# A fast-matrix MLP in an encoder layer: second half product by product, summed in PSUM; first half with the next group's operands combined ahead

## The chip, the cores and the metric

The kernel runs on one core of one Trainium2 chip, in one launch. The metric is device time in microseconds, as the median of several runs. A profile of one execution gives the trace that is read here. The engines are TensorE (PE in the trace; its weight loads are PEld), VectorE (DVE), ScalarE (ACT), GpSimd (POOL) and SyncE (SP), which issues nearly all DMAs here.

## The reference, cut to what matters

One encoder layer on 2048 prompt tokens and 256 sample tokens, width 1024: an adaptive-norm modulation, one input projection, dilated attention on half of the heads, RWKV-7 mixing on the other half, an output projection, and then the MLP that this change is about (`D_FF` is 4096):

```
x = x + gt1 * (concatenate([attn, rw]) @ w_out)
h = rmsnorm(x, g_norm2) * (1 + sc2) + sh2
x = x + gt2 * (square(relu(h @ w_ff1)) @ w_ff2)
```

## The kernel before, in words

All is float32. A product that must be exact enough is made of three float32r matmuls: each operand is split into a high part (a ScalarE copy to float32r) and a low part (the value less the high part), and high*high, high*low and low*high are summed in PSUM.

The kernel has four phases; the last two matter here. `phase_c` makes the output projection, the residual, the second norm, and the first half of the MLP (`h @ w_ff1`). `phase_d` makes the second half (`... @ w_ff2`) and the second residual. Both halves use Winograd's form of Strassen's method: each matrix is cut into 2 x 2 blocks, seven products of block combinations stand in for eight block products, and additions put the results together.

The 2304 tokens are cut into three groups of 768, each of two halves of 384 (`GROUPS`, line 2625). The order in which instructions stand on each engine's queue is written out by a planner (`Pace`, lines 70 to 258): each part of the work is a stream (a generator), which yields what it waits for and which engine it uses next. The planner keeps a rough clock with estimated costs, always lets the stream go on whose next step could start first, and so fixes one order per engine; SP's DMAs are ordered in the same way. On the chip each engine and SP then run their queue strictly in that order, with semaphores for what they wait for. `room(name, n)` stands for one of n buffers of a name coming free, `take` takes one, `drop` gives it back.

**First half, in `phase_c`.** For each group, and for each of 16 passes p (one 128-row block of each half of the 4096 hidden columns), `up_stream` (line 2260) makes the seven products, 12 matmuls of 384 columns each. The moving operands `HS[0..6]` (tiles `hs0h`, `hs0l`, ... in the trace) are combinations of the four blocks of the group's h2 (128 x 1536 in SBUF each), made once per group: `hload_stream` (line 2153) loads the blocks for each of the seven combinations anew from HBM, 14 loads of 768 KB through three buffers `hr`; `hpart_stream` (line 2170) adds or subtracts them on VectorE (seven additions per group) and copies the high part on ScalarE, once the group before has used that operand for the last time; `hlow_stream` (line 2187) makes the low part on VectorE. There is one set of `HS`, shared by the groups. `part_stream` and `low_stream` prepare the weight combinations (`s`, `mh`, `ml`, `mx`, `xn`; lows on GpSimd). `sum_up_stream` (line 2285) reads the products out of PSUM, mostly on VectorE, applies relu and square, and makes the seven left operands of the second half, which go to HBM as `gs`. The four result banks of a pass are used twice within it: products 4, 5 and 6 wait until products 0, 2 and 3 have been read.

**Second half, in `phase_d`.** The inner dimension of each block product (2048 rows) is cut into four quarters q of four 128-row blocks. The loop runs over groups g, then q, then the seven products i (`TURNS`, line 2384): 84 turns. A turn has a left operand (384 tokens x 512 rows, loaded from `gs` as `sr` by `left_load`, split by `left_part` into `s`: high on ScalarE, low on VectorE) and a right operand (512 rows x 512 columns, high and low in a tile `t`, two buffers). `right_load` (line 2419) loads the four blocks of `w_ff2` for each (g, q), 1 MB each, tiles `b`; `right_part` (line 2431) combines them with four VectorE subtractions and copies the seven high parts on ScalarE; `right_low` (line 2490) makes the low parts on GpSimd. As g is the outer loop, all right operands are made three times. `down_stream` (line 2501) runs the turn's 36 matmuls of 512 columns: three PSUM banks (128 tokens each), 12 matmuls per bank. `add_stream` (line 2519) reads each bank and copies it (q = 0) or adds it to the accumulators `acc[0..6]` in SBUF. After the fourth quarter `out_stream` (line 2555) combines the accumulators of the seven products into the four blocks of the result (`acc` + `acc` on VectorE), multiplies by the gate (VectorE), adds the residual `xr` (GpSimd) and stores. `finish_load` (line 2535) loads the gates and the residuals.

Of the kernel before, what the change touches and what calls it, by code (L numbers as in the profile page):

```python
# [18 lines left out]
D = 1024  # L19
# [242 lines left out]
def hymba_layer(ctx, tc, A, out_p, out_s, scratch):  # L262
# [1675 lines left out]
    def phase_c(pc):  # L1938
# [11 lines left out]
        first = ExitStack()  # L1950
# [22 lines left out]
        def gate(i, rg):  # L1973
            z, turn = take(wp, [128, D], FT, f"gate{rg}", 1)
            g = S["gates"]
            dma(z, bass.AP(tensor=g.tensor, offset=g.offset + (i * 2 + rg) * D, ap=[[0, 128], [1, D]]))
            gates[i, rg] = z, turn
# [95 lines left out]
        def sum_stream():  # L2073
            for b in BL:
                for h in range(2):
# [4 lines left out]
                    z, t = take(wp, [128, 512], FT, "z", 2)  # L2080
# [42 lines left out]
        def scale_stream():  # L2123
            for b in BL:
                rg = int(b >= SP // 128)
                yield room("hf", 2), "V"
                hf, t = take(wp, [128, KD, 128], FT, "hf", 2)
# [10 lines left out]
            ended.add("scale")  # L2138

# [12 lines left out]

        def hload_stream():
            for g in range(3):
                for th in range(2):
                    yield (*(lambda b=b: b in hs_ and hs_[b].t is not None for b in GROUPS[g][th]), "S")
                for i, parts in enumerate(MOVING):
                    if i == 4 and not g:
                        yield at("pool"), "S"
                    for j, part in enumerate(parts):  # L2160
                        yield room("hr", 3), "S"
                        z, turn = take(hp, [128, 4, 384], FT, "hr", 3)
                        kh, th = BLOCKS[part.strip("-")]
                        for c0, b0, n in RUNS[g][th]:
                            dma(z[:, :, c0:c0 + n], S["h2"][4 * kh:4 * kh + 4, :, b0:b0 + n].rearrange("k p t -> p k t"))
                        raws["h", g, i, j] = z, turn
                        mark(at("raw", "h", g, i, j), 4200.0)
                        yield

        def hpart_stream():  # L2170
            for g in range(3):
                for i, parts in enumerate(MOVING):
                    yield at("raw", "h", g, i, 0), (lambda: not g or (g - 1, NP - 1, i) in through), "V"
                    z, turn = raws.pop(("h", g, i, 0))
                    for j, part in list(enumerate(parts))[1:]:
                        yield at("raw", "h", g, i, j), "V"
                        y, t1 = raws.pop(("h", g, i, j))
                        tt(y, z, y, OP.subtract if part[0] == "-" else OP.add)
                        drop(turn)
                        z, turn = y, t1  # L2180
                    yield "A"
# [547 lines left out]
```

## Time and profile before

| | |
|---|---|
| median of 3 runs | 4220.1 us (4215.66 to 4223.14) |
| profiled execution, its own time | 4224.25 us |
| its span, first to last instruction | 4222.4 us, mean granted TensorE clock 0.95 |
| TensorE matmul busy | 3861.4 us (91%) |
| VectorE, ScalarE, GpSimd busy | 3218.9 (76%), 1995.5 (47%), 2143.1 us (51%) |
| DMA | 651.33 MB, 154 GB/s over the span |
| passes of the first MLP half | from about 2611 to 3390 us of the span |
| second half | from about 3393 us to the end |

In the rows of the trace, nearly every compute instruction has line L119, since the planner's wrapper issues it; so groups are told apart by their tiles (`out<-in`), their shape and their engine. A group's row gives busy time, mean ns of one, and the idle time of that engine just before such instructions with what ended it. Buffer numbers are left out of tile names. "issue" is time in which the engine waited for nothing that the profile shows.

### The profile page before, as it was taken

What the parts mean: (1) busy time and instruction counts of PE and PEld (TensorE: products, weight loads), DVE (VectorE), ACT (ScalarE), POOL (GpSimd) and SP (SyncE); (2) the same over time, 40 slices, a digit from 0 to 9 for tenths busy, and PEclk for the clock granted to TensorE, in tenths of its full rate; (3) what the DMA queues carried; (4) which work ended last, traced back from release to release, by engine and by line L of the source; (5) the groups of instructions that cost most, each with busy time, mean ns of one, the idle gap of its engine ahead of it and who ended that gap; (6) DMA issues with size and microseconds to landing.
All of it is one profiled execution on the core that took longest, in us unless ns stands there. A gap on an engine that the chain in (4) does not pass through costs nothing.

```text
span 4222.4 us, 77051 instructions
## 1 busy us (share of the span) xinstructions
PE 3861.4 (91%) x28986; PEld 3181.1 (75%) x28986; DVE 3218.9 (76%) x5708; ACT 1995.5 (47%) x4437; POOL 2143.1 (51%) x1760
## 2 busy tenths in 40 slices
PE   8989999997999999999999798997979979889897
PEld 5878878887666666666666577997979967677675
DVE  4898888798668668767667355888888867988978
ACT  5556556555565565566455222333333333333232
POOL 2564442122545645545544444775757745565654
PEclk9999999999899999899799899998989999999999
DMA  6566555454423323324222475546564464454543
GB/s 228 196 223 236 182 193 191 151 195 156 128 75 103 107 61 107 100 69 123 78 64 60 165 247 172 174 166 220 166 211 153 153 217 153 151 190 151 194 151 110
DMA packets 492837, 651.33 MB, mean 154 GB/s; under 512 B 160688, under 2 KB 363440, under 8 KB 491440
## 3 DMA queue, kind: packets, MB, share of 16 engines
q1 hardware_dynamic: 491632, 645.72, 47.4%
q8 instruction: 228, 3.74, 0.4%
q14 instruction: 145, 1.19, 0.1%
q10 hardware_dynamic: 832, 0.69, 0.1%
HBM read 447.83 MB, written 198.46 MB: 153 GB/s over the span
## 4 chain that ended last, share of the span: by engine, by line
PE 42%; DVE 9%; issue 4%; POOL 3%; DMA 2%; ACT 2%; SPq 0%; DVEq 0%; POOLq 0%; ACTq 0%
PE p L119 30%; PE pb L119 5%; PE pc L119 3%; PE ps L119 3%; POOL t L119 2%; DVE acc L119 2%; DMA hr<-scr_h 2%; PE pt L119 1%; DVE s L119 1%; DVE mb L119 1%; DVE hr L119 1%; DVE t L119 0%; DVE b L119 0%; DVE m L119 0%; DMA mx<-scr_mix 0%
## 5 line engine op out<-in xcount | busy, mean ns | idle before, releaser
L119 PE MATMUL p<-t,s 128*128 128x512 f32 x3024 | 720.1, 399 | 94.5 <-POOL t L119 61.4
L119 PEld LDWEIGHTS p<-t,s 128*128 128x128 f32 x3024 | 578.8, 193 | 235.7 <-POOL t L119 75.7
L119 PE MATMUL pin<-hi,whi 128*128 128x386 f32 (+3 forms) x1512 | 495.6, 328 | 4.8 <-ACT praw L327 3.5
L119 PE MATMUL pin<-hi,wlo 128*128 128x386 f32 (+3 forms) x1512 | 481.0, 318 | 1.6 <-POOL wlo L119 1.6
L119 PE MATMUL pin<-lo,whi 128*128 128x386 f32 (+3 forms) x1512 | 481.2, 318 | 0.9 <-DVE lo L119 0.9
L119 POOL TENSOR_TENSOR t<-b,t 128x2048 fp32r<-128x2048 f32 x60 | 294.3, 4906 | 176.7 <-ACT t L119 176.7
L119 ACT ACTIVATE s<-sr 128x1536 fp32r<-128x1536 f32 x84 | 125.0, 1488 | 467.3 <-PE p L119 399.2
L119 PEld LDWEIGHTS pin<-hi,whi 128*128 128x128 f32 x1512 | 289.7, 192 | 15.8 <-issue 6.1
L119 PEld LDWEIGHTS pin<-lo,whi 128*128 128x128 f32 x1512 | 290.7, 192 | 4.4 <-DVE lo L119 1.8
L119 PEld LDWEIGHTS pin<-hi,wlo 128*128 128x128 f32 x1512 | 289.9, 192 | 2.6 <-POOL wlo L119 2.6
L119 PE MATMUL ps<-kz,q 128*128 128x512 f32 (+2 forms) x400 | 272.8, 775 | 0.8 <-DVE st L119 0.6
L119 POOL TENSOR_TENSOR sql<-sq,sqh 128x384 fp32r<-128x384 f32 (+1 forms) x104 | 123.8, 1191 | 289.9 <-DVE sqh L119 239.9
L119 POOL TENSOR_TENSOR wlo<-raw,whi 128x512 fp32r<-128x512 f32 x118 | 180.2, 1531 | 166.6 <-ACT whi L327 161.3
L119 POOL TENSOR_TENSOR x<-x,msk 128x512 f32<-128x512 f32 x144 | 172.2, 1204 | 173.8 <-ACT x L119 156.1
L119 POOL TENSOR_TENSOR sw<-uv,wc 64x128 f32<-64x128 f32 x288 | 121.8, 423 | 244.5 <-DVE uv L119 220.0
L119 DVE CUSTOM_DVE_ANT_0 p<-ps,tb 128x256 f32<-128x256 f32 (+2 forms) x400 | 129.7, 362 | 80.9 <-PE ps L119 53.0
L119 DVE TENSOR_TENSOR acc<-acc,p 128x512 f32<-128x512 f32 x189 | 125.5, 681 | 84.2 <-PE p L119 83.9
L119 ACT ACTIVATE p<-p,st 128x256 f32<-128x256 f32 (+2 forms) x384 | 172.8, 453 | 27.9 <-DVE st L119 26.4
L119 DVE TENSOR_TENSOR s<-sr,s 128x1536 fp32r<-128x1536 f32 x84 | 154.3, 1837 | 37.6 <-ACT s L119 37.6
L119 DVE TENSOR_TENSOR u<-u,p 128x384 f32<-128x384 f32 x192 | 106.4, 554 | 100.3 <-PE p L119 90.2
L119 POOL TENSOR_TENSOR t<-t,t 128x2048 fp32r<-128x2048 f32 x24 | 117.6, 4900 | 109.4 <-ACT t L119 109.4
L119 PE MATMUL pb<-kr,bk 64*128 64x128 f32 x1152 | 156.9, 299 | 0.8 <-DMA bk<-scr_bk 0.3
(446 smaller groups left out, 10952.4 us busy)
## 6 DMA issues: line engine op xcount, KB each, us to landing
scr_gs<-gs SPq DMA_DIRECT2D x336, 192.0 KB
sr<-scr_gs SPq DMA_DIRECT2D x84, 768.0 KB
x<-wff SPq DMA_DIRECT2D x96, 512.0 KB
b<-wff SPq DMA_DIRECT2D x48, 1024.0 KB
whi<-scr_wp SPq DMA_DIRECT2D x54, 512.0 KB
wlo<-scr_wp SPq DMA_DIRECT2D x54, 512.0 KB
hr<-scr_h SPq DMA_DIRECT2D x34, 768.0 KB
raw<-wada SPq DMA_DIRECT2D x83, 256.0 KB
```

The source lines that it names most:

```text
L119: return f(out, *a, **k)
```

## The change: what it does

**Second half.** The loops are turned around: the product i is now the outermost, then the group g, then the quarter q. The right operands of a product (four quarters) are made once and kept for all three groups: five buffers `t`, of which one can be filled ahead, and each of the others once the third group's turn has used the old one. Their blocks are loaded for each product as it needs them, through three buffers `b` (14 block loads per q over the seven products, 56 in all), with 28 VectorE additions. The four quarters of a product are summed in PSUM: the three banks of an (i, g) stay open over four turns and are read once. The combining is done while reading: two accumulators for all tokens (`X`, `W`, nine tiles of 128 x 512 each) hold the partial sums, and products 1, 4, 5 and 6 each finish one block of the result for all groups, which is gated, added to the residual and stored at once. The products come in another order, so `PLACE` and the order of `gs` change with it. The loads of gates and residuals wait for the first product, and residuals come in single tiles with four buffers.

**First half.** For groups 1 and 2, `hload_stream` loads each of the four blocks once, into buffers taken from two pools; `hpart_stream` makes three combinations before the group before has ended (`t1`, `t2`, and b22 - b12 in b12's place) and a fourth, `t4`, after the first operand has been copied; the high-part copies still wait for the last use of the old operand. The buffers for the second pool come from a pool of the output projection (gates, `z`, `hf`), moved to a pool of its own, `zC`, that is closed when the norm is done.

```diff
+        zp = second.enter_context(tc.tile_pool(name="zC", bufs=1, side="right", reuse_waits="tile"))
...
+            yield at("summed"), "V"
+            second.close()
+            late["more"] = pc.enter_context(tc.tile_pool(name="mC", bufs=1, side="right", reuse_waits="tile"))
+            mark(at("more"))
...
+        HR = [("hr", n) for n in ("b11", "b12", "t1")] + [("hm", n) for n in ("b22", "b21", "t2")]
...
+            yield at("more"), "S"
+            for g in (1, 2):
+                if g == 2:
+                    yield at("t4", 1), "S"
...
+                for where, n in HR:
+                    yield room(where, 3), "S"
+                    raws["h", g, n] = take(hp if where == "hr" else late["more"], [128, 4, 384], FT, where, 3)
+                    if n in BLOCKS:
+                        hload(raws["h", g, n][0], g, n)
+                    mark(at("raw", "h", g, n), 4200.0)
+                    yield
...
+            for g in (1, 2):
+                yield (*(at("raw", "h", g, n) for n in ("b11", "b12", "b22", "b21", "t1", "t2")), "V")
+                r = {n: raws.pop(("h", g, n)) for _, n in HR}
+                tt(r["t1"][0], r["b12"][0], r["b11"][0], OP.subtract)
+                yield "V"
+                tt(r["t2"][0], r["b22"][0], r["t1"][0], OP.subtract)
+                yield "V"
+                tt(r["b12"][0], r["b22"][0], r["b12"][0], OP.subtract)
+                yield
+                for i, n in enumerate(("b11", "t2", "b12", "t1", "b21", "t4", "b22")):
+                    if i == 1:
+                        yield room("hr", 3), "V"
+                        r["t4"] = take(hp, [128, 4, 384], FT, "hr", 3)
+                        tt(r["t4"][0], r["b21"][0], r["t2"][0], OP.subtract)
+                        mark(at("t4", g))
+                    yield (lambda: (g - 1, NP - 1, i) in through), "A"
+                    act(HS[i][0], r[n][0], AF.Copy)
...
-        TURNS = [(g, q, i) for g in range(3) for q in range(4) for i in range(7)]
-        acc = [dp.tile([128, 3, 512], FT, name=f"acc{i}") for i in range(7)]
+        TURNS = [(i, g, q) for i in range(7) for g in range(3) for q in range(4)]
+        RIGHT = [("b11",), ("b21",), ("b22", "-b12", "b11"), ("b12", "-b11"), ("b22", "-b12"), ("b22",),
+                 ("b21", "-b22", "b12", "-b11")]
+        DONE = {1: (0, 0), 4: (1, 1), 5: (0, 1), 6: (1, 0)}
+        X, W = (dp.tile([128, 9, 512], FT, name=n) for n in "xw")
...
         def right_part():
+            for i in range(7):
                 for q in range(4):
+                    yield at("raw", i, q, 0), "V"
+                    z, turn = raws.pop((i, q, 0))
+                    for j, part in list(enumerate(RIGHT[i]))[1:]:
+                        yield at("raw", i, q, j), "V"
+                        y, t1 = raws.pop((i, q, j))
+                        tt(y, z, y, OP.subtract if part[0] == "-" else OP.add)
+                        drop(turn)
+                        z, turn = y, t1
+                    yield room("t", 5), "A"
+                    w, t = take(dp, [128, 2, 4, 512], FR, "t", 5)
+                    act(w[:, 0], z, AF.Copy)
...
         def down_stream():
+            for i, g, q in TURNS:
+                yield at("s", i, g, q), at("t", i, q), "P"
...
+                    if q == 0:
+                        yield room("p", 8), "P"
+                        pp[i, g, k] = take(psum, [128, 512], FT, "p", 8)
...
+                        mm(ps, s[:, 0, r, ks], w[:, 0, r], start=q == 0 and r == 0, stop=False, skip_group_check=True)
...
+                if g == 2:
+                    drop(t1)
...
         def out_stream():
+            for i in range(7):
+                for g in range(3):
+                    for k in range(3):
+                        x, w = X[:, 3 * g + k], W[:, 3 * g + k]
+                        yield at("p", i, g, k), "V"
+                        ps, turn = pp.pop((i, g, k))
+                        if i == 0:
+                            copy(x, ps)
+                        elif i == 2:
+                            tt(x, x, ps, OP.add)
+                        elif i == 3:
+                            tt(w, x, ps, OP.add)
+                        if i not in DONE:
+                            drop(turn)
+                            continue
...
+                        tt(o, x if i in (1, 6) else w, ps, OP.add)
+                        if i == 4:
+                            yield "V"
+                            tt(x, x, ps, OP.add)
...
+                        tt(o, o, XS["gate", int(b >= SP // 128)][:, half(h)], OP.mult)
...
+                        (tt if last else gtt)(o, o, z, OP.add)
...
-    PLACE = dict(a11=0, s2=1, a12=2, s3=3, s1=4, s4=5, a22=6)
+    PLACE = dict(a11=0, a12=1, s2=2, s1=3, s3=4, s4=5, a22=6)
```

More of the change, by code (lines that the diff above doesn't have):

```diff
@@ L1973, in gate @@
         def gate(i, rg):
-            z, turn = take(wp, [128, D], FT, f"gate{rg}", 1)
+            z, turn = take(zp, [128, D], FT, f"gate{rg}", 1)
             g = S["gates"]
@@ L2155, in hload_stream @@
                 for th in range(2):
                     yield (*(lambda b=b: b in hs_ and hs_[b].t is not None for b in GROUPS[g][th]), "S")
[L2157 to L2168, printed above, removed]
@@ L2170, in hpart_stream @@
-        def hpart_stream():
[L2171 to L2181, printed above, removed]
-                    act(HS[i][0], z, AF.Copy)
-                    raws["z", g, i] = z, turn
+                for where, n in HR:
[5 more added lines that the diff above has]
+                    yield
@@ L2397, in left_load @@
         def left_load():
-            for g, q, i in TURNS:
+            for i, g, q in TURNS:
                 yield room("sr", 2), "S"
@@ new lines, in right_part, with right_low @@
+                    lows.append((z, turn))
+                    mark(at("th", i, q))
+                    yield
+        lows = []
+        def right_low():
+            for i in range(7):
+                for q in range(4):
+                    yield at("th", i, q), "G"
+                    w = WW[i, q][0]
+                    z, turn = lows.pop(0)
+                    gtt(w[:, 1], z, w[:, 0].bitcast(FT), OP.subtract)
+                    drop(turn)
+                    mark(at("t", i, q))
+                    yield
@@ L2515, in down_stream @@
+                        mm(ps, s[:, 0, r, ks], w[:, 1, r], start=False, stop=False, skip_group_check=True)
+                        mm(ps, s[:, 1, r, ks], w[:, 0, r], start=False, stop=q == 3 and r == 3, skip_group_check=True)
+                    if q == 3:
+                        mark(at("p", i, g, k))
                 drop(t0)
[L2516 removed]
+                if g == 2:
+                    drop(t1)
                 yield
[L2519 to L2533 removed]
@@ L2535, in finish_load @@
         def finish_load():
-            yield "S"
+            yield at("p", 0, 0, 0), "S"
             for rg in range(2):
@@ new lines, in finish_load @@
+            for i, (th, h) in DONE.items():
+                for g in range(3):
+                    for k in range(3):
+                        yield room("xr", 4), at("p", *((i, g - 1, 0) if g else (i - 1, 2, 0))), "S"
+                        z, turn = take(dp, [128, 512], FT, "xr", 4)
+                        dma(z, rows(out_p, out_s, GROUPS[g][th][k])[:, half(h)])
+                        XS[i, g, k] = z, turn
+                        mark(at("xr", i, g, k), 5000.0)
+                        yield
```

220 lines of the change are left out of this document (69 added, 151 removed).

## Prediction, made before the changed kernel was built or run

> **What bounds the kernel now.** I read the stages in the order of the windows first, then the groups of the last stage, then the chain of waits. Columns of the windows: stretch, its length, busy us (and count) of TensorE, weight loads, VectorE, ScalarE, GpSimd, granted clock, DMA share, GB/s.
>
> ```profile
> 2800.00:2850.00 50.00, 50.00 (x289) 50.00 (x288) 43.46 (x55) 19.27 (x32) 35.87 (x23) 1.00 0.51 170
> 2850.00:2950.00 100.00, 76.27 (x389) 73.99 (x389) 80.94 (x90) 36.17 (x55) 55.69 (x34) 0.85 0.69 221
> 3100.00:3200.00 100.00, 77.06 (x395) 74.92 (x394) 82.84 (x89) 37.27 (x56) 55.83 (x34) 0.86 0.60 200
> 3393.40:4222.40 829.00, 720.10 (x3024) 578.76 (x3024) 678.16 (x486) 279.62 (x168) 464.74 (x117) 0.95 0.50 166
> 3450.00:3500.00 50.00, 46.95 (x206) 38.19 (x205) 39.23 (x28) 17.32 (x12) 29.15 (x6) 1.00 0.48 158
> 3600.00:3700.00 100.00, 83.69 (x338) 65.85 (x336) 92.99 (x65) 31.30 (x19) 58.29 (x17) 0.95 0.45 147
> 3400.00:3450.00 50.00, 38.65 (x157) 30.97 (x158) 31.15 (x21) 17.89 (x12) 23.26 (x5) 0.86 0.72 255
> ```
>
> The first half (`phase_c`) is TensorE alone between group changes: 289 matmuls in 50 us, no gap, clock 1.00. At each change of token group a hole opens: 389 and 395 matmuls in 100 us where 578 would fit. A matmul takes 50/289 = 0.173 us there, so the holes cost (189+183) x 0.173 = 64 us. The second half (`phase_d`) is TensorE with gaps everywhere: 3024 matmuls, 720 us busy in 829. Its groups (busy, mean ns, idle before and the releasers):
>
> ```profile
> L119 PE MATMUL p<-t,s 128*128 128x512 f32 x3024 | 720.1, 399 | 94.5 <-POOL t L119 61.4 <-DVE s L119 17.7 <-ACT t L119 15.3
> L119 POOL TENSOR_TENSOR t<-b,t 128x2048 fp32r<-128x2048 f32 x60 | 294.3, 4906 | 176.7 <-ACT t L119 176.7
> L119 DVE TENSOR_TENSOR s<-sr,s 128x1536 fp32r<-128x1536 f32 x84 | 154.3, 1837 | 37.6 <-ACT s L119 37.6
> L119 DVE TENSOR_TENSOR acc<-acc,acc 128x512 f32<-128x512 f32 x63 | 128.5, 2046 | 0.6
> L119 DVE TENSOR_TENSOR acc<-acc,p 128x512 f32<-128x512 f32 x189 | 125.5, 681 | 84.2 <-PE p L119 83.9
> L119 ACT ACTIVATE s<-sr 128x1536 fp32r<-128x1536 f32 x84 | 125.0, 1488 | 467.3 <-PE p L119 399.2 <-issue 56.5 <-DMA sr<-scr_gs 11.6
> L119 POOL TENSOR_TENSOR t<-t,t 128x2048 fp32r<-128x2048 f32 x24 | 117.6, 4900 | 109.4 <-ACT t L119 109.4
> L119 ACT ACTIVATE t<-b 128x2048 fp32r<-128x2048 f32 x60 | 114.3, 1905 | 19.5 <-DVE b L119 16.0 <-DMA b<-wff 3.4
> L119 DVE TENSOR_TENSOR b<-b,t 128x2048 f32<-128x2048 f32 x12 | 63.3, 5274 | 0.0
> L119 DVE COPY acc<-p 128x512 f32<-128x512 f32 x63 | 40.9, 681 | 19.9 <-PE p L119 14.1 <-issue 5.8
> L119 POOL TENSOR_TENSOR acc<-acc,xr 128x512 f32<-128x512 f32 x33 | 53.5, 1621 | 87.5 <-DVE acc L119 87.5
> L119 DVE TENSOR_TENSOR acc<-acc,gate 128x512 f32<-128x512 f32 x36 | 46.4, 1290 | 0.7
> ```
>
> TensorE waits for the low parts of the weights (`t`, GpSimd, 84 of 4.9 us) and, at the end of each group, for VectorE, which is full from 3600 to 3700 (92.99 of 100). In time, TensorE in this half:
>
> ```profile
> 3405.37 0.79 PE L119 MATMUL p<-t,s 128*128 128x512 f32 x1 [15.34 <-ACT t L119]
> 3409.95 10.44 PE L119 MATMUL p<-t,s 128*128 128x512 f32 x36 [3.79 <-POOL t L119]
> 3422.57 41.22 PE L119 MATMUL p<-t,s 128*128 128x512 f32 x180 [2.18 <-POOL t L119]
> 3464.73 16.61 PE L119 MATMUL p<-t,s 128*128 128x512 f32 x72 [0.94 <-POOL t L119]
> 3483.45 41.16 PE L119 MATMUL p<-t,s 128*128 128x512 f32 x180 [2.11 <-POOL t L119]
> ```
>
> A run without a gap gives the floor: (41.22 - 0.39)/179 = 0.228 us a matmul (0.39 is the time of one, in the row of its tile below). One turn (36 matmuls) is 8.2 us, all 3024 are 690 us. And the end:
>
> ```profile
> L119 PE MATMUL p<-t,s x3024: 387/389/795, 3405.4 to 4204.2; 128*128 128x512 f32 x189
> 4217.92 0.69 DVE L119 TENSOR_TENSOR acc<-acc,gate 128x512 f32<-128x512 f32 x1
> 4218.65 0.69 DVE L119 TENSOR_TENSOR acc<-acc,xr 128x512 f32<-128x512 f32 x1
> ```
>
> The last matmul ends at 4204.6, the span at 4222.4: 17.8 us of additions, gates and stores behind TensorE.
>
> On the price of a matmul the Trainium skill (TensorE: Matmul & The Clock Gate, "Wait — 56ns, not 53.3ns?") gives 215.7 ns from start to start for 512 warm columns. By it the floor would be 652 us and the forecast some 37 us lower. These rows show 228 ns at a granted clock of 1.00 with a weight load before each matmul, and the change leaves that pairing alone, so the sum goes by 228.
>
> **The change, second half.** Same 84 turns, same 3024 matmuls, same 84 left loads, ScalarE copies and VectorE lows (`s`). Gone: 56 of 84 right copies (56 x 1.905 = 107 us of ScalarE), 56 of 84 GpSimd lows (56 x 4.9 = 275 us), all 63 `acc+acc` (128.5 us), and 252 readings of PSUM become 72 (9 each for products 0, 2, 3, 1, 5, 6; 18 for product 4): 180 x 0.68 = 123 us of VectorE. The right additions fall from 48 to 28 (2+1+1+3 per q), each between 2.28 and 5.3 us:
>
> ```profile
> L119 DVE TENSOR_TENSOR t<-b,b x12: 2277/5574/5936, 3406.1 to 4129.8; 128x2048 f32<-128x2048 f32 x12
> ```
>
> Added: 8 right loads of 1 MB (56 for 48). VectorE will have 154 + 28 x 2.3 to 5.3 + 72 x 0.68 + 36 x 1.29 = 313 to 398 us, GpSimd 28 x 4.9 + 33 x 1.62 = 191, in about 715: neither can bound. So the stalls that the two set for every turn have no cause left, and TensorE runs on its floor plus four terms:
>
> (a) Start. The same chain as now: first matmul at 3405.4, held 3.8 us by the first GpSimd low and at a low clock; its first turn ends at 3420.4 (3409.95 + 10.44), 15.0 us for the turn. I keep both, with 4 us either way as bounds (that wait gone, or met twice); the gates' loads now leave SP's queue ahead of the third left load (they wait for the first product), which can only help.
>
> (b) 83 warm turns: 83 x 36 x 0.228 = 681 us.
>
> (c) Stalls, unseen in this trace. A left operand needs its buffer (freed when the turn before last ends), 1.49 of ScalarE and 1.76 of VectorE: 3.3 us in a turn of 8.2, so 4.9 are spare. A GpSimd low can hold the VectorE step back by all its 4.9 us (the addition above takes 2.28 us at best and 5.57 at the median, beside GpSimd), which just fits. So a left stall needs a right addition as well: I take 8 us over all switches. At a switch of product, right operands of q 1 to 3 can only be copied as the old ones are used up, one per turn. For product 6 (four blocks each) the operands of q 2 and 3 still need 6 of their 8 MB then, 6.3 MB, and beside them come five left loads (3.9) and some 2 MB of outputs: 12.2 MB, in the 49 us to the turn that needs the last, less 9 for addition, copy and low: 40 us, 305 GB/s. The most that the windows show is 255 (3400 to 3450). At that it takes 48 us: 8 us late. Product 2 (three blocks) needs some 200 GB/s and fits. So (c) is 16 us; the bounds are 0, and 50 where each load also waits behind another in SP's queue (rival B).
>
> ```profile
> sr<-scr_gs SPq DMA_DIRECT2D x84, 768.0 KB
> b<-wff SPq DMA_DIRECT2D x48, 1024.0 KB
> ```
>
> By the Trainium skill (DMA: Bandwidth & Descriptors, "Specifications") a core gets about 358 GB/s from HBM; by that the 305 would fit, and (c) would be 8. No window here comes near it.
>
> (d) Tail. After the last matmul one tile of 128x512 is left: three VectorE steps of 0.69 with 0.2 between, then the store, which now takes 4222.4 - 4219.3 = 3.1 us: 5.4 for 17.8. The tiles before it end 2.7 us earlier each (12 matmuls) and are gone by then.
>
> End: 3405.4 + 15.0 + 681 + 16 + 5.4 = 4123 on the old time axis, 99 us before 4222.4.
>
> On SP the loads of `xr` become one tile each (36, as now) with four buffers. Waiting there they would hold up the left loads behind them; the cover is the left load's 13 us from issue to need (two turns less 3.3), against 5.1 to 6.4 for the loads of the same 768 KB in the chain below, so a wait of 6 is free.
>
> **First half.** The holes are this chain:
>
> ```profile
> 2865.31 5.06 DMA hr<-scr_h
> 2879.92 5.77 DMA hr<-scr_h
> 2887.50 6.42 DMA hr<-scr_h
> 2894.01 1.77 DVE hr L119
> 2895.80 1.49 ACT hs5h L119
> 2897.32 1.77 DVE hs5l L119
> 2899.13 206.38 PE p L119 x1175
> ```
>
> Fourteen loads through three buffers, seven additions, then copy and low. For groups 1 and 2 the change makes that four loads and four additions, three of them before the group ends, and the loads a group ahead (16 x 7 x 12 x 0.173 = 233 us). What stays at the change: seven copies (1.49, ScalarE 19 of 50 us busy, hidden), seven lows and one addition, 8 x 1.76 = 14 us on VectorE, in a stretch from 3.6 us after the old group's last pass begins to 27 us (a pass of seven products is 14.6 us; operand 6 is due two passes less one product on). VectorE is busy 43.46 of 50 there, so 23.4 us leave 3 idle. 14 don't fit into 3 without something being late: 11 us. The lows themselves have 9 us to spare (12.5 from the freeing of an operand to its use, less 3.3), the weight combinations up to a pass, but the PSUM readings of products 1 to 3 only 4 (their banks are needed again for products 4 to 6). I take 6 us of stall per change: half, since lateness is shared. Bounds: 0, and 19 (all 14 and the three earlier additions unhidden). So 64 - 12 = 52 us are won.
>
> The move of gates, `z` and `hf` to a pool of their own, which is closed before the new buffers are taken, costs nothing: their last writer is the scaling stream, which ends before the first pass; the new loads have the first group's 230 us as cover. If that cover went, they would come as late as now.
>
> **Sum.** 4222.4 - 99 - 52 = 4071.4 span. The profiled run took 4224.25 (1.85 outside the span), 4.15 above the median of the runs: 4071.4 + 1.85 - 4.15 = 4069 us.
>
> **Rivals.**
> A. *VectorE takes the loads' place at the group changes.* For: 43.46 of 50 busy, 11 us too much. Against: two thirds of that are spare elsewhere. At 19 us a change 64 - 38 = 26 are won: 4095. Chance 0.13.
> B. *Right operands are late at every switch*: three buffers, loads in line with left loads and outputs. For: 255 GB/s at most. Against: only products 2 and 6 need more than two blocks per q. With 50 us of stalls: 4103. Chance 0.17.
> C. *No stall worth naming*: (c) 0, 0 to 3 at a change: 4069 - 16 - 6 to 12 = 4041 to 4047. Chance 0.09.
> D. *The transfers bound the second half, and it is slower than before.* Its traffic is 84 x 0.786 + 56 x 1.049 + 72 x 0.262 + 1.0 = 145 MB. If DMA gives no more than between 3600 and 3700, 147 GB/s, it lasts 986 us instead of 829: 157 more, less 52: 4325. It decides from under 145/(829 + 52) = 165 GB/s, just the present mean of 166. For: the present rate is that. Against: it is what is asked for now, at half the DMA share; 255 and 221 stand in the windows. Chance 0.05, of which 0.02 lies near no change.
> E. *The plan comes out otherwise than the change says* (the operands ahead are loaded late, a queue's order undoes them): the holes stay: 4121. Chance 0.03.
>
> **How the numbers follow.** The forecast has 0.53: 4069, its own range 4055 to 4085. To hold 8 in 10 I go down to C (4041) and up over A and B nearly to both together (4130): 4041 to 4125. Faster by over 0.2% (8 us, about what a measurement of this kernel can tell) has 0.95: all but D; 0.02 within, 0.03 slower.
>
> **What would show it.** Right: 28 lows `t` and copies instead of 84; idle before the 512-column matmuls under 50 us with start included; their busy time near 697 (3024 x 0.228 + some 7 of low clock); VectorE at about half in the second half; over 540 matmuls per 100 us at the group changes; the span ends within 6 us of the last matmul. Wrong: idle before `p` put to `b` loads or ACT `t` (B), to DVE `hs` or to PSUM readers (A), or DMA share above 0.8 all along (D).

## The result, and the profile after

| | before | after |
|---|---|---|
| median | 4219.8 us (4215.66 to 4223.14, 4 runs) | 4089.4 us (4087.93 to 4096.51, 4 runs) |
| ratio, 95% interval | | 0.9695 [0.9678, 0.9712] |
| profiled run, its span | 4224.25, 4222.4 us | 4087.93, 4086.1 us |

The change made the kernel 130 us faster; 151 were forecast (4069, with 4055 to 4085 as its own range). To see where, I cut both profiled spans at two matmuls of the groups: the first and the last start with the operand `hs6h` (the end of each pass). Duration (min/median/max, ns), first and last start; the kernel before:

```profile
L119 PE MATMUL p<-hs6h,xn x96: 334/334/346, 2679.7 to 3389.7; 128*128 128x384 f32 x96
```

and after, with the second half's matmuls:

```profile
L119 PE MATMUL p<-hs6h,xn x96: 334/334/450, 2670.9 to 3357.4; 128*128 128x384 f32 x96
...
L119 PE MATMUL p<-t,s x3024: 387/389/795, 3373.1 to 4080.6; 128*128 128x512 f32 x189
```

| stretch of the profiled span | before | after | won | forecast |
|---|---|---|---|---|
| up to the groups (first `hs6h`) | 2679.7 | 2670.9 | 8.8 | 0 |
| groups: first to last `hs6h` | 710.0 | 686.5 | 23.5 | 52 |
| second half: from there to the end | 832.7 | 728.7 | 104.0 | 99 |

The first stretch takes between 2662 and 2693 us over the profiled runs below, with hardly anything changed in it (nothing in its first 2350 us): that is variation from run to run, and totals carry it. The other two repeat: four kernels with the changed first half gave 686.5, 687.1, 687.0 and 687.2 for the groups, three with the old one 710.0, 709.9 and 710.2. What follows is read from these two. (The expectations of the runs mostly speak of a first half counted from the first matmul of the output projection, 1004.7 us in the changed kernel: that has 316 to 328 us of the varying part in it.)

**Second half.** Its groups in the page of the changed kernel (busy us, mean ns | idle before, releaser), and TensorE in time:

```profile
L119 PE MATMUL p<-t,s 128*128 128x512 f32 x3024 | 692.8, 391 | 30.4 <-ACT t L119 15.3
L119 DVE TENSOR_TENSOR s<-sr,s 128x1536 fp32r<-128x1536 f32 x84 | 174.5, 2079 | 311.1 <-ACT s L119 310.8
L119 POOL TENSOR_TENSOR t<-b,t 128x2048 fp32r<-128x2048 f32 x28 | 138.7, 4958 | 317.7 <-ACT t L119 316.6
```

```profile
3373.07 0.80 PE L119 MATMUL p<-t,s 128*128 128x512 f32 x1 [15.32 <-ACT t L119]
3377.68 18.49 PE L119 MATMUL p<-t,s 128*128 128x512 f32 x73 [3.81 <-POOL t L119]
3399.49 182.44 PE L119 MATMUL p<-t,s 128*128 128x512 f32 x792 [3.33 <-DVE s L119]
3582.71 16.66 PE L119 MATMUL p<-t,s 128*128 128x512 f32 x72 [0.78 <-DVE s L119]
3601.05 8.46 PE L119 MATMUL p<-t,s 128*128 128x512 f32 x36 [1.69 <-DVE s L119]
3611.56 90.08 PE L119 MATMUL p<-t,s 128*128 128x512 f32 x396 [2.05 <-DVE s L119]
3701.86 212.48 PE L119 MATMUL p<-t,s 128*128 128x512 f32 x936 [0.21 <-DVE s L119]
3916.01 81.94 PE L119 MATMUL p<-t,s 128*128 128x512 f32 x360 [1.68 <-DVE s L119]
3999.50 81.44 PE L119 MATMUL p<-t,s 128*128 128x512 f32 x358 [1.55 <-DVE s L119]
```

Idle time before these matmuls fell from 94.5 to 30.4 us: 15.3 at the start and 3.8 after the first matmul, both as before, and 11.3 in seven waits for left lows `s`. From 3701.86 on there are 936 matmuls with no gap at all. Of the 104 us won, 64 are this idle time, 27 are the matmuls' own busy time (720.1 to 692.8, at a mean granted clock of 0.99 for 0.97), and 13 are the tail, which is now three VectorE steps of 0.69 and a store: 5.5 us from the last matmul's start to the end.

**First half.** The holes at the group changes are narrower, not closed (columns: stretch, length, busy us and count of TensorE, weight loads, VectorE, ScalarE, GpSimd, clock, DMA share, GB/s):

```profile
2750.00:2800.00 50.00, 50.00 (x288) 50.00 (x288) 43.24 (x56) 20.05 (x35) 38.52 (x25) 1.00 0.49 164
2800.00:2850.00 50.00, 45.02 (x253) 44.70 (x252) 43.80 (x50) 22.41 (x34) 34.78 (x22) 0.95 0.46 147
2850.00:2950.00 100.00, 87.80 (x474) 86.36 (x473) 86.13 (x100) 35.36 (x59) 61.17 (x38) 0.92 0.51 169
3050.00:3150.00 100.00, 89.91 (x481) 88.44 (x480) 90.22 (x100) 41.98 (x65) 65.31 (x41) 0.93 0.41 136
```

Against 289 in 50 us, 36 + 104 and 97 matmuls are missing: at 0.173 us each 24.2 and 16.8 us, 41 where the kernel before lost 64. That is the whole of the 23.5 won. Only 17.2 and 10.1 us of them are idle time. The other 14 are slow matmuls behind the waits, where the granted clock fell to 0.92 and 0.93: a 384-column matmul in the rows below took up to 543 ns on average, and 336 elsewhere. What TensorE waits for has changed too. In the first hole, from 2800 to 2920:

```profile
L119 PE MATMUL p<-hs5h,ml 128*128 128x384 f32 x16 | 5.9, 439 | 8.1 <-DVE u L119 8.1
L119 PE MATMUL p<-hs4h,mh 128*128 128x384 f32 x11 | 4.2, 452 | 3.3 <-ACT m L119 3.3
L119 PE MATMUL p<-hs4h,ml 128*128 128x384 f32 x8 | 3.7, 543 | 5.0 <-ACT m L119 5.0
```

`m` (ScalarE) and `u` (VectorE) are the readings of earlier products' PSUM banks, which products 4 and 5 need again. No load of `hr` is left in these waits. From VectorE's queue, two of the seven lows and what stands ahead of the reading that released the 8.1 us:

```profile
2845.68 2.82 DVE L119 TENSOR_TENSOR hs1l<-hm,hs1h 128x1536 fp32r<-128x1536 f32 x1
2848.42 2.83 DVE L119 TENSOR_TENSOR hs2l<-hr,hs2h 128x1536 fp32r<-128x1536 f32 x1
...
2871.01 2.83 DVE L119 TENSOR_TENSOR hr<-hr 128x1536 f32<-128x1536 f32 x1
2873.87 2.70 DVE L119 TENSOR_TENSOR hm<-hm,hr 128x1536 f32<-128x1536 f32 x1
2876.50 1.75 DVE L119 TENSOR_TENSOR hr<-hm,hr 128x1536 f32<-128x1536 f32 x1
2878.17 1.14 DVE L119 TENSOR_TENSOR gs<-gs 128x384 f32<-128x384 f32 x2
2879.22 0.55 DVE L119 TENSOR_TENSOR u<-m,p 128x384 f32<-128x384 f32 x1
```

The three rows of `hr` and `hm` are the combinations for group 2, which nothing needs for another 220 us. They were put into the hole of group 1, as soon as their blocks had come.

### The profile page after: what moved, and what is told of

It is laid out like the page before. It is cut to its first block, busy times and chain, and to the rows that moved or that the text cites. A ratio compares the mean times of both kernels' runs of the same rounds, so it can differ in the third digit from the quotient of the medians.

```text
span 4086.1 us, 76583 instructions
## 1 busy us (share of the span) xinstructions
PE 3825.0 (94%) x28986; PEld 3168.5 (78%) x28986; DVE 2863.5 (70%) x5439; ACT 1892.2 (46%) x4381; POOL 1884.5 (46%) x1704
## 4 chain that ended last, share of the span: by engine, by line
PE 55%; DVE 10%; DMA 3%; issue 3%; POOL 2%; ACT 2%; SPq 0%; DVEq 0%; POOLq 0%; ACTq 0%
PE p L119 32%; PE pb L119 10%; PE ps L119 5%; PE pc L119 5%; PE pt L119 2%; DMA b<-wff 2%; DVE s L119 1%; DVE mb L119 1%; PE pin L119 1%; POOL t L119 1%; POOL x L119 1%; DVE m L119 1%; DVE b L119 1%; DVE gs L119 1%; DMA hr<-scr_h 0%
## 5 line engine op out<-in xcount | busy, mean ns | idle before, releaser
L119 PE MATMUL p<-t,s 128*128 128x512 f32 x3024 | 692.8, 391 | 30.4 <-ACT t L119 15.3
L119 PEld LDWEIGHTS p<-t,s 128*128 128x128 f32 x3024 | 570.2, 189 | 152.9 <-ACT t L119 15.6
L119 DVE TENSOR_TENSOR s<-sr,s 128x1536 fp32r<-128x1536 f32 x84 | 174.5, 2079 | 311.1 <-ACT s L119 310.8
L119 POOL TENSOR_TENSOR t<-b,t 128x2048 fp32r<-128x2048 f32 x28 | 138.7, 4958 | 317.7 <-ACT t L119 316.6
L119 ACT ACTIVATE p<-p,st 128x256 f32<-128x256 f32 (+2 forms) x384 | 172.8, 453 | 28.5 <-DVE st L119 26.7
L119 POOL TENSOR_TENSOR o<-o,xr 128x512 f32<-128x512 f32 x33 | 63.2, 1916 | 189.9 <-DVE o L119 179.5
L119 PEld LDWEIGHTS pb<-kr,bk 64*128 64x128 f32 x1152 | 136.8, 203 | 18.1 <-issue 8.6
```

Source lines behind the costliest of these rows:

```text
L119: return f(out, *a, **k)
```

## The experiments

The kernel before was timed beside each set of runs (medians 4221.1 to 4224.5 us). Ratios are to it, with their 95% interval; the last two columns are the stretches of the table above.

| kernel | median us | ratio | groups | second half |
|---|---|---|---|---|
| the changed kernel | 4089.4 | 0.9695 [0.9678, 0.9712] | 686.5 | 728.7 |
| e1 second half's change alone | 4119.8 | 0.9747 [0.9726, 0.9767] | 709.9 | 729.8 |
| e2 first half's change alone | 4199.5 | 0.9940 [0.9925, 0.9956] | 687.1 | 832.4 |
| e3 combinations in mid-group | 4097.6 | 0.9702 [0.9685, 0.9719] | 695.5 | 730.4 |
| e4 readings ahead of lows | 4086.6 | 0.9669 [0.9651, 0.9686] | 679.8 | 730.4 |
| e5 lows left out | 4070.7 | 0.9637 [0.9614, 0.9659] | 659.3 | 733.0 |
| e6 = e4, squares on ScalarE | 4077.2 | 0.9656 [0.9635, 0.9677] | 670.8 | 728.7 |
| e7 right lows on VectorE | 4079.4 | 0.9661 [0.9637, 0.9685] | 687.0 | 711.6 |
| e8 first right operand in four pieces | 4098.6 | 0.9694 [0.9672, 0.9717] | 687.2 | 724.4 |
| e9 = e6, combinations spread | 4081.1 | 0.9658 [0.9632, 0.9685] | 679.0 | 729.8 |
| e10 = e9, e7 and e8 | 4057.3 | 0.9604 [0.9582, 0.9626] | 677.8 | 706.1 |
| e11 the kernel before, right lows on VectorE | 4193.9 | 0.9929 [0.9904, 0.9953] | 710.2 | 808.1 |
| e12 = e10, weights' lows at the change on VectorE | 4048.3 | 0.9593 [0.9577, 0.9610] | 674.0 | 706.2 |

### The two halves alone

e1 keeps the old `hload_stream` and `hpart_stream`, e2 the old `phase_d`. The cores of the two edits, against the changed kernel:

```diff
# e1
-            for g in (1, 2):
...
-                for where, n in HR:
...
+            for g in range(3):
+                for i, parts in enumerate(MOVING):
# e2
-        TURNS = [(i, g, q) for i in range(7) for g in range(3) for q in range(4)]
+        TURNS = [(g, q, i) for g in range(3) for q in range(4) for i in range(7)]
```

> The second half changed, the first half as before. Theory (the halves add; the trace of the changed kernel shows its second half 104 us shorter, from the last matmul of the first half to the end: 728 for 832): 4219.8 - 104 = 4116 us, ratio 0.975. Forecast on record: 99 us, 4121. Rival (the second half is only that fast because the first half, too, delivers or frees something earlier): the gain is under 95 us, above 4125.

> The first half changed, the second half as before. Theory from the trace of the changed kernel (the holes at the group changes shrink only from 64 us to about 41, and the start of the phase wins 3): 25 to 28 us, so 4193 us, ratio 0.994. Forecast on record: 52 us, 4168. Rival (part of the 32 us by which the first half ended earlier in the profile is the earlier end of the unchanged phases, so it is less): 4205 if only one change wins.

By medians e1 won 104.7 us and e2 25.0, together 129.6; the whole change 130. The halves neither help nor hurt each other; the stretches say the same (each edit moves its own to within 1.1 us of the changed kernel's, and leaves the other where it was before). The shortfall against the forecast lies in the first half.

### Where the first half's rest went: the combinations

```diff
# e3, in hpart_stream, ahead of the three combinations
+                yield (lambda: (g - 1, 8, 0) in through), "V"
```

> As the changed kernel, but the next group's three combinations on VectorE wait until the ninth pass of the running group, so that group 2's are not made inside the hole at the first group change. Theory P (place: the three combinations of 1.8 to 2.8 us stand ahead of the PSUM readings in the first hole and cost the wait of 8.1 us before product 5): the wait falls to about 1 as at the second change, 4089 - 8 = 4081. Theory W (work: VectorE has simply too much to do around a change, with or without them): under 3 us, 4086 to 4089.

The wait before product 5 fell from 8.1 to 2.3 us, and new holes opened where the combinations now stand, in the ninth pass of each group:

```profile
2700.00:2750.00 50.00, 44.80 (x245) 44.48 (x245) 40.75 (x50) 16.27 (x29) 30.75 (x21) 0.93 0.44 145
2960.00:3010.00 50.00, 44.81 (x245) 44.49 (x244) 40.00 (x50) 16.29 (x30) 30.63 (x21) 0.93 0.44 146
```

245 matmuls for 289 is 7.6 us each; the groups took 9.0 us more, not less. So three additions in one go (2.9, 1.8 and 1.8 us here) did not fit into the ninth pass either, a quiet one.

### The order of the queue, and the amount of work

e4 puts the readings of a product's PSUM banks ahead of the next copies and lows. e5 leaves out the lows of the moving operands of groups 1 and 2 (their tiles keep what stood there), so its time holds seven VectorE steps less at each change. e6 is e4 with the three `square(relu())` of a pass taken from VectorE to ScalarE.

```diff
# e4, in the list of streams: a rank behind that of the readings
-                     (hpart_stream, 0), ... (hlow_stream, 0),
+                     (hpart_stream, "hold"), ... (hlow_stream, "hold"),
# e5, in hlow_stream
-                    tt(l, z, h.bitcast(FT), OP.subtract)
+                    if g == 0:
+                        tt(l, z, h.bitcast(FT), OP.subtract)
# e6, three times a pass
-                stt(a22, u3, 0.0, u3, OP.max, OP.mult)
+                act(u3, u3, AF.Relu)
+                act(a22, u3, AF.Square)
```

> As the changed kernel, but in the planner the streams of the operand preparation (high copies, low parts, combinations) start 70 ns later in rank, so that they come behind the PSUM readings and the rest where both could start at the same time. No instruction is added or removed. Theory O (order: the holes come from PSUM readings that stand behind lows on VectorE and behind high copies on ScalarE, while the lows have 9 us to spare): the waits of TensorE for ACT m and DVE u at both changes (17 and 10 us, and the slow clock after them) fall to a few us, 4089 - 20 to 35 = 4054 to 4069. Theory W (work: 14 us of VectorE that do not fit): the wait only moves to the low parts, DVE hs, and the time stays at 4083 to 4089.

> As the changed kernel, but the seven low parts of the moving operands are not made for groups 1 and 2 (those groups use group 0's low parts): 14 VectorE instructions of 1.75 to 2.8 us left out, the high copies, combinations and loads stay. Theory W (at a change VectorE has too much work, whatever the order): the waits of TensorE for ACT m and DVE u at both changes fall from 17 and 10 us to a few us where group 2's combinations stand (up to 8 at the first change, under 3 at the second), and the time falls by 15 to 30 us, to 4060 to 4075. Rival (the high copies on ScalarE, held until the old operand's last use, hold up the copy m behind them by themselves): the waits for ACT m stay at 5 and 3 us per change, and the time stays above 4080.

> The fourth run's order (PSUM readings first), and besides the three relu-and-square steps per pass that VectorE makes in one instruction of 0.56 to 1.07 us go to ScalarE as two of 0.5 each, in all passes. That takes some 2 us of 12.6 from VectorE in each pass of 14.6. Theory W: in the two passes around a change 4 us less of the 14 that do not fit, so holes of 10 us of idle shrink to about 5, and the slow clock behind them goes: 4086 - 12 = 4074. Rival (ScalarE's longer chain delays the readings as much): no change, 4083 to 4090.

With the readings first (e4) TensorE waited for the lows instead; from its waits over the first half (us in total, times, longest):

```profile
PE p L119 <- DVE hs3l L119: 11.1, 2, 5.6
PE p L119 <- DVE u L119: 10.5, 6, 4.3
PE p L119 <- DVE hs2l L119: 5.3, 2, 2.7
PE p L119 <- DVE hs5l L119: 3.0, 2, 1.6
```

6.7 us were won (686.5 to 679.8), but with the readings first it was the lows that came late, and some readings (`u`) still did. Without the lows (e5) 27.2 us were won, and half of each change's hole or more was gone:

```profile
2800.00:2850.00 50.00, 50.00 (x289) 49.97 (x288) 43.22 (x56) 22.66 (x37) 35.19 (x24) 1.00 0.53 170
2850.00:2950.00 100.00, 91.34 (x510) 90.70 (x509) 85.61 (x101) 40.96 (x68) 72.66 (x45) 0.95 0.52 173
3050.00:3150.00 100.00, 98.50 (x564) 97.82 (x563) 87.97 (x109) 47.32 (x75) 72.27 (x47) 1.00 0.52 167
```

Missing are 68 and 14 matmuls: 11.8 and 2.4 us for 24.2 and 16.8. What stays in the first hole, 7.5 us before product 5 behind `u`, stands behind group 2's combinations again; the second hole, with no combinations in it, is nearly closed. e6 won 15.7 us against the changed kernel, 9.0 of them over e4: the amount of VectorE's work, then, more than its order.

### The second half's stalls: VectorE and GpSimd

```diff
# e7, in right_low
-                    yield at("th", i, q), "G"
+                    yield at("th", i, q), "V"
-                    gtt(w[:, 1], z, w[:, 0].bitcast(FT), OP.subtract)
+                    tt(w[:, 1], z, w[:, 0].bitcast(FT), OP.subtract)
```

> As the changed kernel, but in the second half the low parts of the right operands are made on VectorE (2.3 us each) instead of GpSimd (4.6 to 6.6). Theory L (VectorE's s steps and GpSimd's lows take turns on something they share: s takes 1.75 alone and up to 6.0 beside a low): the wait after the first matmul falls from 3.8 to 1.5 us, s steps stay under 3.5 us and the DVE s waits fall from 11.3 to under 6: 4089 - 7 = 4082. Rival Q (the stalls come from VectorE's queue, where an addition waits for its block and s stands behind it): the waits stay at 11 or grow as VectorE gets 64 us more to do: 4087 to 4095.

In the changed kernel, the stall of 1.69 us at 3601.05 builds up like this:

```profile
3592.78 1.92 ACT L119 ACTIVATE t<-b 128x2048 fp32r<-128x2048 f32 x1 [9.45 <-DVE b L119]
3594.60 1.47 ACT L119 ACTIVATE s<-sr 128x1536 fp32r<-128x1536 f32 x1
3594.77 4.61 POOL L119 TENSOR_TENSOR t<-b,t 128x2048 fp32r<-128x2048 f32 x1 [0.87 <-ACT t L119]
3596.10 4.90 DVE L119 TENSOR_TENSOR s<-sr,s 128x1536 fp32r<-128x1536 f32 x1 [3.36 <-ACT s L119]
```

ScalarE's copy of a right operand waits for its addition and holds the left copy behind it; then GpSimd's low begins, at 3594.77, and ends at 3599.38. VectorE's low begins inside it and ends at 3601.00, 1.62 us after GpSimd: hardly anything of its own 1.75 us was done before.

Four of the seven waits end behind such a low, which took 4.9 us or more: 3.33, 0.78, 1.69 and 2.05 us, 7.9 in all. In the other three (0.21, 1.68 and 1.55 us) the low took its own 1.75 us, but stood in VectorE's queue behind an addition that waited for a block of the right operand, as here ahead of the wait at 3999.50:

```profile
3995.49 2.29 DVE L119 TENSOR_TENSOR b<-b 128x2048 f32<-128x2048 f32 x1 [2.26 <-DMA b<-wff]
3997.69 1.75 DVE L119 TENSOR_TENSOR s<-sr,s 128x1536 fp32r<-128x1536 f32 x1
```

With GpSimd's lows gone (e7):

```profile
L119 PE MATMUL p<-t,s 128*128 128x512 f32 x3024 | 689.0, 390 | 17.1 <-ACT t L119 15.6 <-DVE t L119 1.5
L119 DVE TENSOR_TENSOR s<-sr,s 128x1536 fp32r<-128x1536 f32 x84 | 150.9, 1797 | 276.6 <-ACT s L119 276.2
L119 DVE TENSOR_TENSOR t<-b,t 128x2048 fp32r<-128x2048 f32 x28 | 65.6, 2346 | 14.3 <-ACT t L119 13.7
```

Every stall but the start's is gone. From the first matmul's start to the last one's are 690.1 us, which is the floor of 3024 x 0.228 = 689.5. Loads, additions and outputs are as many as before and VectorE has 65.6 us more to do, so it was not the amount of VectorE's work. That the three waits behind late blocks went too is not explained by GpSimd alone: the planner wrote the queues anew, with some left copies and lows ahead of right ones, and no run separates the two.

### The start

```diff
# e8: the first right operand, load, copy and low in four pieces, the lows on VectorE
+                        if i + q == 0:
+                            for r in range(4):
+                                dma(z[:, r], A["wff2"][f0 + r, :, half(h)])
```

> As the changed kernel, but the second half's first right operand is loaded in four pieces of 256 KB ahead of the first left load, copied in four pieces, and its low part made in four pieces on VectorE. Theory S (the 15.3 us before the first matmul and the 3.8 us after it are the first 1 MB load, 8.5 us, its copy, 1.9, and its low, 4.6): the first matmul starts some 5 us earlier and runs on: 4089 - 8 = 4081. Rival (the wait is for the whole tile, or the left operand is as late): under 3 us, 4086 to 4090.

The wait behind the first matmul fell from 3.8 to 1.1 us, but that matmul came later, 20.0 us after the first half's last one and not 15.7: I had moved the right load ahead of the left one, and ScalarE now waited 20.78 us for `sr`. The second half is still 4.3 us shorter, since the wait of 3.3 us after the second turn has gone as well. In e10, with the left load ahead again, the gap is 12.9.

### Spread, and all together

e9 takes the next group's additions one per pass, after the products 3, 7, 11 and 13 of a group, on top of e6. Besides, it has a fourth buffer `hr` and one `z` fewer. e10 adds e7 to it, and e8 with the left load first.

```diff
# e9, in hpart_stream, one such line ahead of each addition
+                yield (lambda: (g - 1, 3, 0) in through), "V"
```

> The changed kernel, with the first half's passes in the order of the two runs before (the readings of a product's PSUM banks issued ahead of the lows of the next operand, and the squares on ScalarE), and with the next group's three combinations taken one at a time, after the products 3, 7 and 11 of a group, the fourth low beside product 13, instead of in one stretch. A fourth buffer for the combined operand, one buffer fewer for the reading's scratch tile. The second half is that of the changed kernel. Theory S (what is left of the first half's holes is three additions in one stretch, 2.8, 2.7 and 1.8 us, in front of readings with about 4 us to spare; one addition fits): the stretch from the first matmul of the first half's groups to the last low falls from 991.5 us to 975-985, no wait there above 3 us, and the total is 4062-4072. Theory T (every addition opens a stall wherever it is put, since the passes have no room on VectorE at all): the stretch stays at 988-995, total 4075-4085.

> The kernel of the run before this one with, in the second half, all lows of the right operands on VectorE (none on GpSimd) and the first right operand loaded, copied and subtracted in four pieces behind the left operand's load. Theory S with sharing (the second half's stalls come from VectorE and GpSimd subtracting at once): the stretch from the last matmul of the first half to the end is 705-712 us against 728.7 in the changed kernel, the total 4043-4055, about 1% less than the changed kernel. Rival (the gains lie over each other: with the second half's operands earlier, the first half's end and the switch wait on something else): the stretch 715-728, total 4058-4075.

```profile
2650.00:2700.00 50.00, 49.79 (x286) 49.47 (x285) 37.71 (x47) 28.44 (x54) 35.55 (x25) 1.00 0.51 162
2750.00:2800.00 50.00, 48.84 (x281) 48.52 (x280) 36.55 (x45) 27.11 (x51) 34.22 (x23) 1.00 0.52 171
2850.00:2900.00 50.00, 41.18 (x208) 40.10 (x207) 40.69 (x39) 27.36 (x47) 33.59 (x19) 0.83 0.56 179
3100.00:3150.00 50.00, 41.18 (x215) 40.11 (x214) 40.34 (x39) 29.28 (x49) 34.88 (x20) 0.86 0.40 128
```

In e9 the holes lose 81 and 74 matmuls (14.0 and 12.8 us), and passes with an addition in them 3 to 8 (0.5 to 1.4 us). In e6 the same two stretches lose 74 and 66. So the holes are no narrower though the additions have left them; why they are a little wider is not shown. Single additions open small stalls of their own, and the groups took 679.0 us, 8.2 more than in e6: the theory that one addition fits without cost fell. e10's second half took 706.1 us, as expected; its total, 4057.3, lies just above the range expected of it, and its groups were hardly shorter than e9's (677.8).

### Is it sharing that slowed the old second half?

e11 is e7's edit made to the kernel before.

> The kernel before, with one edit: the lows of the second half's right operands, which were GpSimd's, on VectorE (84 of them at about 2.3 us as in the run of the changed kernel with that edit). Theory L (what slowed the old second half was VectorE and GpSimd sharing, not the sums that VectorE took per product): the stretch from the last matmul of the first half to the end falls from 832.7 us to under 790, total under 4180. Rival M (it was the amount of VectorE's work per pass: with some 190 us more on VectorE it has 680 us and more of the stretch's 690 us of matmul time): the stretch stays within 20 us of 832 or grows, total 4205-4260.

```profile
L119 PE MATMUL p<-t,s 128*128 128x512 f32 x3024 | 716.0, 398 | 70.7 <-DVE t L119 34.9 <-DVE acc L119 19.8 <-ACT t L119 15.3
L119 DVE TENSOR_TENSOR t<-b,t 128x2048 fp32r<-128x2048 f32 (+1 forms) x72 | 163.5, 2284 | 0.4
L119 DVE TENSOR_TENSOR acc<-acc,acc 128x512 f32<-128x512 f32 x63 | 55.5, 889 | 0.3
L119 DVE TENSOR_TENSOR t<-t,t 128x2048 fp32r<-128x2048 f32 x24 | 54.8, 2282 | 0.0
```

24.6 us were won in the second half: between the two theories' figures, and neither holds alone. VectorE was busy 681.5 us, as much as before (678.2), with the 84 lows more. Those are the last row and, but for 12 additions of the same shape, the second: 84 x 2.284 = 191.9 us. Summed by rows (whose sums lie above the busy time, as rows overlap a little), the other 486 instructions took 517 us where they had taken 698. So 181 us of VectorE's rows in the kernel before went with GpSimd's lows (73 of it in the 63 `acc+acc`, 128.5 us there and 55.5 here), nearly as much as the lows cost when VectorE makes them itself. That done away with, VectorE's own amount of work still made TensorE wait, 34.9 and 19.8 us. The change's other 79 us came only with the change itself: the sums of products in PSUM, a third of the right operands instead of all, and the shorter tail (13 us). No run separates the first two.

### Sharing at the group changes

```diff
# e12, in low_stream
-                    yield at("wh", g, p, i), "G"
+                    early = g > 0 and p in (1, 2)
+                    yield at("wh", g, p, i), "V" if early else "G"
```

> The kernel that had all the edits (next group's additions one at a time, squares on ScalarE, second half's right lows on VectorE, first right operand in four pieces), with one more: the lows of the weights' operands of the second and third pass of groups 1 and 2 (14 of 128x512 per change) on VectorE instead of GpSimd. In that kernel, from 2849 to 2862 us of the run with the additions spread, GpSimd's lows took 2.8 us instead of 1.3 to 1.6, and VectorE's lows hs3l and hs4l 2.84 and 2.39 instead of 1.75. Theory G (the rest of the holes is VectorE and GpSimd sharing too): VectorE takes 14 x 0.69 = 10 us per change more and gets about as much back, the copies get their lows sooner; the wait before product 4 behind the copy m (6.7 us, twice) falls under 3, the stretch from the first matmul of the first half's groups to the last low falls from 994.4 to 980-988, the total to 4043-4052. Rival V (VectorE's amount of work in these 27 us is what is too much, however it is shared): the wait stays or grows, the stretch is 992-1005, the total 4055-4068.

The holes narrowed from 215 and 216 matmuls in 50 us (e10) to 231 and 229, by 2.8 and 2.2 us, and the longest wait for `m` fell from 6.7 to 5.0; the groups became 3.8 us shorter. The stretch as the expectation counts it, 990.7 us, lies between what the two theories expected: sharing is a part of what is left there, and the edit doesn't show how large. The two medians don't settle it either: 15.2 of the 18.9 us between the two profiled spans lie ahead of the groups, and the intervals overlap.

Against the changed kernel, e12 is about 1% faster (0.9593 for 0.9695, the intervals apart): of 43.5 us between the spans 12.5 lie in the groups, 22.5 in the second half and 8.5 ahead of both. e6's first half with e10's second, which the stretches suggest as better still (670.8 and 706.1), was not run.

## Why the forecast was right, and where it was wrong

**Sign and bound: right.** The second half was TensorE held up by the per-turn work of GpSimd and VectorE, and that went. In the first half's holes the loads were the last to end, and no load is left in them; but VectorE's work stood right behind.

**Floor and start, (a) and (b): right.** 15.3 us of gap, 3.8 behind the first matmul, and 0.228 us a matmul: e7's 690.1 us against 689.5. By the figure of the Trainium skill (TensorE: Matmul & The Clock Gate, "Wait — 56ns, not 53.3ns?") the floor would be an estimated 652; no run here came near it.

**Stalls, (c): 11.3 us for 16; one half right, the other far too large.** The 8 us for left lows that GpSimd holds back measured 7.9, as e7's section shows; 3.3 of them came in the third turn, where no right operand needs an addition, so that the size fits so well is luck in part. The 8 us at the switch to product 6 rested on 255 GB/s as the most that DMA gives, and that was a reading over 50 us. Shorter stretches of the kernel before (first two lines) show more, and so does the changed kernel (last two, the second of them the 40 us ahead of the last addition for product 6):

```profile
3390.00:3430.00 40.00, 18.68 (x70) 14.54 (x70) 23.64 (x16) 9.97 (x6) 14.06 (x3) 0.74 0.84 299
3396.00:3416.00 20.00, 6.84 (x19) 5.12 (x20) 11.64 (x5) 4.81 (x4) 4.51 (x1) 0.55 1.04 383
3885.00:3925.00 40.00, 38.32 (x169) 31.32 (x168) 32.12 (x21) 8.78 (x6) 13.01 (x6) 1.00 0.96 336
3956.00:3996.00 40.00, 40.00 (x179) 33.10 (x178) 27.23 (x15) 11.18 (x7) 17.65 (x4) 1.00 0.77 264
```

At 336 GB/s the 12.2 MB take 36 us, within the 40. Right blocks were late all the same: the wait there was 1.55 us, for a left low behind an addition that waited for its block, and 1.68 us at 3916 have the same cause. So rival B's mechanism is there, at 3.4 us in all. DMA was busy for 0.77 of these 40 us, and the late block's load was issued only at 3988.44, 7 us before the addition; whether the three buffers or the loads in front held it back is left open. The Trainium skill's 358 GB/s (DMA: Bandwidth & Descriptors, "Specifications") was a better guide than 255, and a sentence of the prediction gave 8 us by it. But that no window of the kernel before comes near it was wrong: 383 GB/s over 20 us lie above it, and the measurement decides.

**Tail, (d): right**, 5.5 for 5.4. **Second half in sum:** 104 for 99, the 5 us being (c).

**First half: the step that failed is "I take 6 us of stall per change: half, since lateness is shared".** It measured 24.2 and 16.8, and 23.5 us were won for 52. Rival A, VectorE in the loads' place at 19 us a change (4095, chance 0.13), is what happened: 20.5 us a change on average. Of the signs that the prediction named, over 540 matmuls per 100 us at the group changes did not come (474 and 481). Four things were wrong in the step:
- "Shared" assumed that the spare time of lows, weight combinations and readings could be lent from one to another. On VectorE's queue they stood one behind another: in the changed kernel the readings stood behind lows and combinations, and their 4 us ran out first; with the readings first (e4) it was the lows that ran out.
- The lows' price. 1.76 us each was right only for some; hs1l and hs2l took 2.8 in the first hole, and each ended 1.6 us after a GpSimd low that had begun before it. Leaving all seven out (e5) won 13.6 us a change, more than the 12.3 us that the prediction counted for them, not half.
- The three early combinations were taken as done "before the group ends", at no price. They were done early indeed, but for group 2 at the start of the group before, in the other hole; and neither place tried instead (e3, e9) was free.
- Idle time was taken for the whole price of a stall. It was 17.2 and 10.1 us; the slow matmuls behind it, 7 us a change, stand nowhere in the step.

**The sum:** span 4086.1 for 4071.4: +28.5 in the groups, -5.0 in the second half, -8.8 ahead of both. The rest of the 20 us is the profiled run, which lay 1.5 us below its median and not 4.15 above. That the total came no further off is luck in part: the 8.8 us ahead of both halves are variation, and they and the second half's 5 hide half of the miss in the groups.

## What to carry to other kernels

When a wait is taken away, count what else the same engine must do in those very microseconds, and price the excess in full: work moved "ahead" must have a named place with room, and a planner that takes the first free one may choose the busiest. A busy engine in a profile is not always an engine at work: VectorE's rows grew where GpSimd's instructions ran, so compare an operation's mean with its own minimum before calling the engine full. And the highest rate that a window shows is a mean over its length (255 GB/s over 50 us were 383 over 20), and no ceiling unless something waited for it at that rate.

## What the runs showed of the hardware that was not expected

- **VectorE waits for the whole of a GpSimd subtraction, not for a share of it.** Beside the stall shown above, the next one ends the same way: GpSimd from 3605.29 for 4.60, VectorE's low from 3606.62 for 4.89, its end 1.62 us behind GpSimd's, and hs1l and hs2l in the first hole do the same. It goes both ways (GpSimd's low took up to 6.58 us for 4.6). Reads from PSUM into VectorE kept their 0.68 us throughout. The Trainium skill (SBUF — State Buffer, "SBUF: two separate sides") says this of the port pair that the two engines have in common: an exclusive lock, held for the whole instruction. These rows agree with it.
- **The size of it:** 181 us of VectorE's rows in the old second half. The 84 lows given to GpSimd there, at 4.9 us each, freed VectorE of next to nothing: it waited nearly as long as it would have worked on them (191.9 us).
- **DMA** moved 383 GB/s over 20 us in the kernel before and 336 over 40 us in the changed one, where windows of 50 us had shown 255.
